# Four edits to a hybrid attention and GLA encoder kernel: norms stored as rows, a bank for P4, combines ahead of slots, and an alternating middle

## The chip, the cores and the metric

The kernel runs on one core of a Trainium2 chip. The metric is the device time in microseconds (us) of one launch. TensorE (PE in the profile) multiplies and accumulates into PSUM, of which this kernel uses eight banks; VectorE (DVE), ScalarE (ACT) and GpSimd (POOL) do the elementwise work; SyncE (SP) and GpSimd issue DMAs. Each engine works through its own queue in order.

## The reference

Two layers work on x of 512 tokens by 2048 features, all in fp32. Cut to what matters:

```python
def hybrid_layer(x, w_in, w_out, ...):
    z = rmsnorm(x, g_pre) @ w_in
    gq, gk, gv, gg, ga, aq, ak, av, ag = split_columns(z)   # GLA: q, k 512 wide, v, gate 1024; attention: 4 x 1024
    log_a = log_sigmoid(ga @ w_alpha + b_alpha) / 16
    o_gla = gla_chunk_causal(gq, gk, gv, log_a)             # 4 heads, state over 8 chunks of 64 tokens
    o_gla = rmsnorm(o_gla, g_gla) * silu(gg)                # per head
    o_att = chunk_band_attention(aq, ak, av, rel_bias)      # 8 heads, own chunk and the 8 before it
    o_att = rmsnorm(o_att, g_att) * silu(ag)                # per head
    y = concatenate([o_gla, o_att]) @ w_out
    return x + rmsnorm(y, g_post)
```

1/rms of a token multiplies the token's whole row of z, so the kernel multiplies unnormed x by the weights and applies 1/rms to the products later: as a number per partition where tokens lie on partitions, and as a row along the free dimension where features do.

## The kernel before

**Operands in two parts.** fp32 values are split in a high part that TensorE multiplies at full rate and a low part. For a chunk of weights, `high` casts the tile (`wh`, ScalarE, L195) and `low` subtracts (`wl`, VectorE, L199). Each product of two values is three matmuls: high by high, high by `wl`, low by `wh`.

**Pairs of output blocks.** Most of the two projections is done by `fast_gemm`, two output blocks of 512 columns at a time, by seven half-size products P1 to P7 in place of eight, each over four chunks of the inner dimension. A chunk of one product is 12 matmuls of 128x512. A layer has seven pairs: GG, AV, QK01 with QK23, QK45 with QK67, GK with GQ, GV, and, at the layer's end, the pair W23 (blocks 2 and 3 of the output projection), which is called the end pair here (`end=True`). The order of products is P1, P5, a middle of P6 and P3, P7, P2, P4; in the end pair P1, P2, P5, the middle, P7, P4. The other blocks (AG0, AG1, output blocks 0 and 1) go through `std_gemm`; output block 1 is done for the first 256 tokens before the end pair and for the others behind it.

**Banks.** A pair has two accumulators, X and Y, of two banks each (one per 128 tokens, `t`). P1, P6, P7 and P4 add into X; P5, P3 and P2 into Y, except in the end pair, where P2 has two auxiliary banks (Z). P1, P5 and P2 start a new sum (`starts`). After P1, P5 and P6 the accumulator is copied to SBUF on ScalarE (`copies`, L347 with 1/rms, L349 without). After P3, P7 and P2 a combine on VectorE (L356 with 1/rms, L358 and L360 without) reads the accumulator and one of the copies and gives a block of the result. P4 goes on adding to P7's sum in X, and that sum is its block of the result with no combine. In a pair of the usual order X is read by P7's combine while P2 runs; in the end pair P4 follows P7 at once.

**What the weights need first.** P5, P6 and the end pair's P4 add a loaded tile to the sum H (L190), P7 subtracts (L192), and P2 adds once more (L204), all on VectorE ahead of the cast. Weight tiles come through SyncE's queue into rings of four buffers (`raw`, `H`, `sa`, `wh`; `wl` has three).

**Tasks beside the stream.** The attention heads, GLA heads, sums and the next layer's preparation are tasks. `pace` runs pieces of them between products, and `until(condition)` runs them until a condition holds. The result of each block goes to a consumer: `kq_consume` for GK and GQ, `gv_consume` for GV. Both take slots in SBUF that are free only once certain attention heads are done, so they call `until` (head 6 and head 4), which emits those heads' instructions at this place. A scheduler orders each engine's instructions when the program is built; the order does not change afterwards.

**1/rms.** `token_norms` computes it for half of the tokens (two columns of 128 partitions), in GpSimd's power (L432), and stores each column to DRAM with a transfer of 128 single numbers on GpSimd's queue (L514), eight in all. `norm_row` reads the numbers back as a row, broadcast to all partitions, where features lie on partitions.

Of the kernel before, what the change touches and what calls it, by code (L numbers as in the profile page):

```python
# [11 lines left out]
ALU = mybir.AluOpType  # L12
# [3 lines left out]
P = 128  # L16
L = 2
S = 512
# [16 lines left out]
def hybrid_trunk(  # L35
# [65 lines left out]
    fac_d = [dram([P, 1024], f"fac{l}") for l in range(L)]  # L101
    r_d = [dram([S, 1], f"r{l}") for l in range(L)]

# [24 lines left out]
    W23 = (NB_IN + 2, NB_IN + 3)  # L128
    MIDDLE = [("P6", 0), ("P3", 0), ("P6", 1), ("P3", 1), ("P6", 2), ("P6", 3), ("P3", 2), ("P3", 3)]

# [199 lines left out]
    def fast_gemm(l, pair, consume, rate=0.0, skip=0, feature_major=False, after=None, end=False, scaled=True):  # L330
# [5 lines left out]
        if end:  # L336
            target["P2"] = "Z"
        prod = PROD_END if end else PROD
# [24 lines left out]
        def finished(k, t):  # L363
            x_, y_ = acc["X"][t], acc["Y"][t]
            if k == "P3":
                consume(1, 0, t, None, combine(y_, 0, t, keep["x"][t], 1, ALU.subtract))
            elif k == "P7":
                consume(1, 1, t, None, combine(x_, 1, t, keep["p5"][t], -1, ALU.add))
            elif k == "P2":
                consume(0, 0, t, None, combine(acc[target[k]][t], 0, t, keep["p1"][t], 1, ALU.add))  # L370
            elif k == "P4":
                consume(0, 1, t, x_, None)
# [31 lines left out]
        for k, c in prod:  # L404
# [5 lines left out]
            if c == 3:  # L410
                if k == "P1":
                    copies("p1", acc["X"])
                elif k == "P5":
                    copies("p5", acc["Y"])
                elif k == "P6":
                    copies("x", acc["X"])
                else:
                    for t in range(2):
                        finished(k, t)
            if after is not None:  # L420
                after(k, c)
# [80 lines left out]
    def token_norms(l, half, xs):  # L502
# [8 lines left out]
        nc.vector.tensor_tensor(out=norm[l][:, 2, cols], in0=ss, in1=r, op=ALU.mult)  # L511
        for j in range(2):
            t = 2 * half + j
            nc.gpsimd.dma_start(r_d[l][t * P : (t + 1) * P, :], inv_rms(l, t))  # L514
        normed.add((l, half))
        yield

    def norm_row(l, tok, n):
        z = t2((tok.stop - tok.start,))
        nc.sync.dma_start(z[0:n], r_d[l][tok, :].rearrange("s o -> o s").partition_broadcast(n))  # L520
        return z
# [140 lines left out]
    def layer(l):  # L662
# [26 lines left out]
        def forget_gate():  # L689
# [13 lines left out]
            until_normed(1)  # L703
            row = norm_row(l, slice(0, S), 96)
            nc.vector.tensor_tensor(out=raw[0:96, 1, :], in0=ps[0:96, :], in1=row[0:96, :], op=ALU.mult)
# [232 lines left out]
        def qk_consume(p):  # L938
            sets = {}

            def f(j, h, b, src, comb):
# [9 lines left out]
                else:  # L951
                    nc.vector.tensor_tensor(
                        out=z, in0=z, in1=norm_row(l, hs, P).unsqueeze(1).to_broadcast([P, 2, 256]), op=ALU.mult
                    )
# [25 lines left out]

        def kq_consume(j, h, t, src, comb):
            if j:
                if not gqT:
                    until(lambda: 6 in heads_done)
                    gqT.extend(slot(tag, [2, 512]) for tag in ("g12", "g13"))
                tasks.insert(0, transpose_q(2 * h + t, settled(src, comb)))
                return
            if not kdh:
                until(lambda: "done" in fgate)
                kdh.extend(slot(tag, [2, 512], F32R) for tag in ("g8", "g11"))  # L990
                kdl.extend(slot(tag, [2, 512], F32R) for tag in ("g14", "g15"))
            z = settled(src, comb)
            if comb is None:
# [166 lines left out]

        def gv_consume(j, h, t, src, comb):
            if (j, h) not in gvh:
                until(lambda: 4 in heads_done)
# [4 lines left out]
            else:  # L1168
                split(gvh[j, h][:, t, :], gvl[j, h][:, t, :], settled(src, comb))
            if h and t:  # L1170
# [176 lines left out]
```

## Time and profile before

| | |
|---|---|
| Median of 3 runs | 1682.63 us (1678.63 to 1688.18) |
| Profiled execution | 1680.65 us, of which the span 1678.9 |
| Mean granted TensorE clock | 0.994 |
| TensorE busy | 1635.4 us (97% of the span), 9026 matmuls and transposes |
| VectorE, ScalarE, GpSimd busy | 1223.9, 900.0, 173.8 us |
| DMA | 470.64 MB, mean 280 GB/s |

A row of the timeline reads: start in us from the span's beginning, duration, engine, line, operation, output and input tiles, shape, how many such instructions in a row; in brackets the idle time before it and what ended it. Matmuls are pipelined, so the duration of one (0.39 us for 128x512) is longer than the distance from one start to the next. A row of the waits reads: engine and line, what it waited for, total us, times, longest. A row of the stretches gives, for each engine, busy time and count, then the granted clock of TensorE, the mean busy share of the DMA engines, and GB/s.

### The profile page before, as it was taken

The numbers are of one execution on the slowest core, as the hardware profiler recorded it, in microseconds if no ns is written. First come the engines' busy times: TensorE is split into PE (matmuls) and PEld (weight loads), VectorE is DVE, ScalarE is ACT, GpSimd is POOL, SyncE is SP. The second block draws the span as 40 slices with busy tenths as digits, with TensorE's granted clock in tenths as the row PEclk, the third lists the DMA queues.
The fourth block names the chain that finished last, engine by engine and source line by source line (L and its number), as shares of the span: only waits on it lengthen the run. The fifth ranks groups of instructions, "written<-read, shape, count | busy, mean of one in ns | idle before, by whom it ended". The sixth has DMA issues, their size and how long they took to land.

```text
span 1678.9 us, 24925 instructions
## 1 busy us (share of the span) xinstructions
PE 1635.4 (97%) x9026; PEld 1396.3 (83%) x9026; DVE 1223.9 (73%) x1587; ACT 900.0 (54%) x1495; POOL 173.8 (10%) x264
## 2 busy tenths in 40 slices
PE   9999999999999999999999999999999999999987
PEld 7888889999987877687887878899999878776776
DVE  7567777877876885688785676768778677856875
ACT  7444544565666544554774454445666565435542
POOL 1210000000100101311121000000010001013101
PEclk9999999999999999999999999999999999999999
DMA  9988786858767787898799597968586778868984
GB/s 380 315 300 323 275 309 227 300 193 305 259 216 263 271 307 254 298 371 306 222 299 396 198 334 260 320 216 290 199 309 238 242 264 287 293 234 308 352 300 181
DMA packets 150683, 470.64 MB, mean 280 GB/s; under 512 B 16532, under 2 KB 35348, under 8 KB 150560
## 3 DMA queue, kind: packets, MB, share of 16 engines
q1 hardware_dynamic: 127408, 389.36, 67.3%
q0 software_dynamic: 22432, 78.41, 12.3%
q8 instruction: 71, 1.16, 0.3%
q10 hardware_dynamic: 720, 1.28, 0.2%
q14 instruction: 52, 0.43, 0.1%
HBM read 396.88 MB, written 72.11 MB: 279 GB/s over the span
## 4 chain that ended last, share of the span: by engine, by line
PE 82%; DMA 9%; DVE 5%; issue 2%; ACT 1%; POOL 0%; SPq 0%; DVEq 0%; ACTq 0%; POOLq 0%
PE mm L396 41%; PE mm L386 18%; PE mm L314 14%; DMA raw<-in_w_dram 3%; PE ax L865 2%; DVE wl L199 2%; DMA t<-fg 2%; DMA sa<-S 1%; DMA sg<-in_x_dram 1%; PE ax L1027 1%; PE ax L848 1%; DMA S<-g 1%; PE ax L696 1%; PE ax L1061 1%; DMA g<-in_x_dram 1%
## 5 line engine op out<-in xcount | busy, mean ns | idle before, releaser
L396 PE MATMUL mm<-wh,sa 128*128 128x512 f32 x1536 | 486.2, 392 | 3.1 <-DMA sa<-S 1.8
L195 ACT CAST wh<-raw 128x1024 fp32r<-128x1024 f32 x256 | 269.4, 1054 | 267.6 <-PE mm L396 98.8
L199 DVE TENSOR_TENSOR wl<-raw,wh 128x1024 fp32r<-128x1024 f32 x256 | 311.2, 1219 | 74.1 <-PE mm L396 19.5
L195 ACT CAST wh<-H 128x1024 fp32r<-128x1024 f32 x224 | 234.8, 1051 | 216.4 <-PE mm L396 114.7
L396 PEld LDWEIGHTS mm<-wh,sa 128*128 128x128 f32 x1536 | 288.1, 188 | 66.2 <-issue 4.9
L199 DVE TENSOR_TENSOR wl<-H,wh 128x1024 fp32r<-128x1024 f32 x224 | 272.6, 1220 | 90.2 <-PE mm L396 40.2
L396 PE MATMUL mm<-wl,sa 128*128 128x512 f32 x768 | 300.5, 391 | 4.6 <-DVE wl L199 4.6
L386 PE MATMUL mm<-sa,wh 128*128 128x256 f32 x1280 | 238.0, 285 | 0.0
L386 PEld LDWEIGHTS mm<-sa,wh 128*128 128x128 f32 x1280 | 200.3, 191 | 0.5
L396 PE MATMUL mm<-wh,a 128*128 128x512 f32 x576 | 183.9, 393 | 2.1 <-DVE t L356 2.1
L386 PE MATMUL mm<-sa,wl 128*128 128x256 f32 x640 | 181.3, 283 | 0.1
L314 PE MATMUL mm<-wh,a 128*128 128x512 f32 x512 | 171.3, 398 | 3.2 <-DVE g L1206 1.1
L396 PEld LDWEIGHTS mm<-wl,sa 128*128 128x128 f32 x768 | 144.3, 188 | 36.1 <-DVE wl L199 7.5
L190 DVE TENSOR_TENSOR H<-H,raw 128x1024 f32<-128x1024 f32 x120 | 145.8, 1220 | 10.0 <-DMA raw<-in_w_dram 8.3
L432 POOL TENSOR_TENSOR sm<-sm,mhalf 128x4 f32<-128x4 f32 (+2 forms) x40 | 58.4, 1459 | 708.7 <-DVE sm L875 458.9
L192 DVE TENSOR_TENSOR raw<-H,raw 128x1024 f32<-128x1024 f32 x56 | 68.6, 1225 | 84.2 <-DMA raw<-in_w_dram 84.0
L396 PEld LDWEIGHTS mm<-wh,a 128*128 128x128 f32 x576 | 107.3, 188 | 24.8 <-DVE t L356 2.4
L386 PEld LDWEIGHTS mm<-sa,wl 128*128 128x128 f32 x640 | 122.4, 191 | 0.4 <-DVE wl L199 0.3
L314 PEld LDWEIGHTS mm<-wh,a 128*128 128x128 f32 x512 | 96.8, 189 | 26.4 <-DVE g L1206 2.0
L396 PE MATMUL mm<-wl,a 128*128 128x512 f32 x288 | 112.6, 391 | 0.0
L314 PE MATMUL mm<-wl,a 128*128 128x512 f32 x256 | 101.2, 395 | 3.6 <-DVE wl L199 3.6
L386 PE MATMUL mm<-a,wh 128*128 128x256 f32 x512 | 94.7, 284 | 0.0
(202 smaller groups left out, 2349.6 us busy)
## 6 DMA issues: line engine op xcount, KB each, us to landing
raw<-in_w_dram SPq DMA_DIRECT2D x320, 512.0 KB, 5.4
sa<-S SPq DMA_DIRECT2D x192, 512.0 KB, 4.6
H<-in_w_dram SPq DMA_DIRECT2D x56, 512.0 KB, 4.6
sa<-A SPq DMA_DIRECT2D x48, 512.0 KB, 5.5
S<-g POOLq DMA_DIRECT2D x32, 512.0 KB, 8.8
oS<-g POOLq DMA_DIRECT2D x32, 512.0 KB, 6.4
sa<-oS SPq DMA_DIRECT2D x32, 512.0 KB, 5.3
sg<-t POOLq DMA_DIRECT2D x32, 256.0 KB, 6.0
```

The lines of the kernel that those rows point to most:

```text
L190: nc.vector.tensor_tensor(out=h, in0=h, in1=r, op=ALU.add)
L192: nc.vector.tensor_tensor(out=r, in0=h, in1=r, op=ALU.subtract)
L195: last_cast[0] = nc.scalar.copy(self.wh, src).ins
L199: last_low[0] = nc.vector.tensor_tensor(out=self.wl, in0=self.src, in1=self.wh.bitcast(F32), op=ALU.subtract).ins
L314: mm = nc.tensor.matmul(pss[o], a[:, part, t], rhs[:, kk, :], start=(i == 0 and kk == 0 and m == 0), stop=(i == n - 1 and kk == 1 and m == 2),
L386: nc.tensor.matmul(dst, lhs[:, kk, f], a[:, part, tok], start=(fresh and kk == 0 and m == 0 and ft % 2 == 0), stop=(c == 3 and kk == 1 and ...
L396: nc.tensor.matmul(out_ps[t], a[:, part, tok], rhs[:, kk, :], start=(fresh and kk == 0 and m == 0), stop=(c == 3 and kk == 1 and m == 2), ...
L432: nc.gpsimd.tensor_tensor(out=out_r, in0=v, in1=mhalf[:, : v.shape[-1]], op=ALU.pow)
L696: nc.tensor.matmul(ps[0:96, half * 256 : (half + 1) * 256], wga[kt // 10][:, kt % 10, :], op[:, i, (kt % 2) * 256 : (kt % 2 + 1) * 256], s ...
L848: nc.tensor.transpose(ps[:, j * P : (j + 1) * P], self.prob[i][:, j * P : (j + 1) * P], ident)
L865: nc.tensor.matmul(o, self.pt[i][:, j * P : (j + 1) * P], av[hd // 4, j // 2][:, j % 2, (hd % 4) * P : (hd % 4 + 1) * P], start=(j == 0), ...
L1027: nc.tensor.matmul(self.ps_u[cc][:, tt * 256 : (tt + 1) * 256], ops[cc][i][0], ops[cc][i][1], start=(i == 0), stop=(i == 2),)
```

## The change

There are four edits.

1. `token_norms` transposes the two columns of 1/rms on TensorE into a 2x128 tile in an auxiliary bank, copies it on VectorE to SBUF, and stores it with one transfer of two rows of 128 numbers: four transfers instead of eight. `norm_row` reads one or two halves, each with its own transfer.
2. In the end pair P4 starts a new sum in Y instead of adding to X. After P7 X is copied by ScalarE (two copies), and P4's block is made by a combine on VectorE (two) of Y and those copies.
3. `kq_consume` and `gv_consume` run the combine (`settled`) first, and only then call `until` and take their slots.
4. The middle goes P6 0, P3 0, P6 1, P3 1, P6 2, P3 2, P6 3, P3 3 in all pairs; before, it was P6 2, P6 3, P3 2, P3 3 in its second half.

```diff
-    r_d = [dram([S, 1], f"r{l}") for l in range(L)]
+    r_d = [[dram([2, P], f"r{l}{half}") for half in range(2)] for l in range(L)]
...
-    MIDDLE = [("P6", 0), ("P3", 0), ("P6", 1), ("P3", 1), ("P6", 2), ("P6", 3), ("P3", 2), ("P3", 3)]
+    MIDDLE = [(p, c) for c in range(4) for p in ("P6", "P3")]
...
         if end:
-            target["P2"] = "Z"
+            target.update(P2="Z", P4="Y")
+            starts.append("P4")
...
             elif k == "P2":
                 consume(0, 0, t, None, combine(acc[target[k]][t], 0, t, keep["p1"][t], 1, ALU.add))
+            elif k == "P4" and end:
+                consume(0, 1, t, None, combine(y_, 1, t, keep["x"][t], 1, ALU.add))
             elif k == "P4":
                 consume(0, 1, t, x_, None)
...
                     for t in range(2):
                         finished(k, t)
+                    if k == "P7" and end:
+                        copies("x", acc["X"])
...
-        for j in range(2):
-            t = 2 * half + j
-            nc.gpsimd.dma_start(r_d[l][t * P : (t + 1) * P, :], inv_rms(l, t))
+        ps = aux()
+        nc.tensor.transpose(ps[0:2, 0:P], r, ident)
+        row = t2((P,))
+        nc.vector.tensor_copy(row[0:2], ps[0:2, 0:P])
+        nc.gpsimd.dma_start(r_d[l][half], row[0:2])
...
-    def norm_row(l, tok, n):
-        z = t2((tok.stop - tok.start,))
-        nc.sync.dma_start(z[0:n], r_d[l][tok, :].rearrange("s o -> o s").partition_broadcast(n))
+    def norm_row(l, halves, n):
+        z = t2((256 * len(halves),))
+        for i, half in enumerate(halves):
+            nc.sync.dma_start(
+                z[0:n, i * 256 : (i + 1) * 256], r_d[l][half].rearrange("a b -> (a b)").partition_broadcast(n)
+            )
         return z
...
         def kq_consume(j, h, t, src, comb):
+            z = settled(src, comb)
             if j:
                 if not gqT:
                     until(lambda: 6 in heads_done)
                     gqT.extend(slot(tag, [2, 512]) for tag in ("g12", "g13"))
-                tasks.insert(0, transpose_q(2 * h + t, settled(src, comb)))
+                tasks.insert(0, transpose_q(2 * h + t, z))
                 return
...
-            z = settled(src, comb)
...
         def gv_consume(j, h, t, src, comb):
+            z = settled(src, comb)
             if (j, h) not in gvh:
                 until(lambda: 4 in heads_done)
...
-                split(gvh[j, h][:, t, :], gvl[j, h][:, t, :], settled(src, comb))
+                split(gvh[j, h][:, t, :], gvl[j, h][:, t, :], z)
```

How the edits move instructions is seen in the queues of three engines. The lines of the changed file lie 1 to 11 further down (L360 becomes L361, L1206 becomes L1217, L396 becomes L399). Tile names carry running numbers, which differ between the two programs.

VectorE in the end pair of layer 0, where P7 passes to P4. The first row is `wl` of P4's chunk 1; before:

```order
L199 TENSOR_TENSOR wl_7782<-H_7202,wh_7766 128x1024
L360 TENSOR_TENSOR t_1517_7808<-ev_7554,mm_7291 128x512
L199 TENSOR_TENSOR wl_7801<-H_7228,wh_7785 128x1024
L1206 TENSOR_TENSOR g_1518_7810<-t_1517_7808,t_1409_7289 128x512
L360 TENSOR_TENSOR t_1520_7814<-ev_7556,mm_7292 128x512
L1206 TENSOR_TENSOR g_1521_7816<-t_1520_7814,t_1409_7289 128x512
L199 TENSOR_TENSOR wl_7832<-H_7273,wh_7804 128x1024
L199 TENSOR_TENSOR wl_7856<-raw_7806,wh_7834 128x1024
```

and now:

```order
L199 TENSOR_TENSOR wl_7791<-H_7211,wh_7775 128x1024
L361 TENSOR_TENSOR t_1521_7817<-ev_7563,mm_7300 128x512
L199 TENSOR_TENSOR wl_7810<-H_7237,wh_7794 128x1024
L1217 TENSOR_TENSOR g_1522_7819<-t_1521_7817,t_1413_7298 128x512
L361 TENSOR_TENSOR t_1524_7823<-ev_7565,mm_7301 128x512
L199 TENSOR_TENSOR wl_7845<-H_7282,wh_7813 128x1024
L1217 TENSOR_TENSOR g_1525_7825<-t_1524_7823,t_1413_7298 128x512
L199 TENSOR_TENSOR wl_7869<-raw_7815,wh_7847 128x1024
L1243 SCALAR_TENSOR_TENSOR g_1358_7071<-g_1341_7013,sm_7854,g_1358_7071 128x1024
L1243 SCALAR_TENSOR_TENSOR g_1359_7072<-g_1453_7475,sm_7854,g_1359_7072 128x1024
L199 TENSOR_TENSOR wl_7893<-raw_7849,wh_7871 128x1024
L359 TENSOR_TENSOR t_1548_7923<-mm_7302,ev_7829 128x512
```

P7's two combines (L360, now L361) and P4's `wl` tiles keep their order, but the second L1206 now follows P4's last `wl`. The combine of P4 (L359) is new; it stands behind two `wl` tiles of output block 1 and two operations of the tokens' finish (L1243).

TensorE in the GK, GQ pair of layer 0, behind the last matmul of P7. L826 to L848 and L890 belong to attention heads; rows of L396 (L399) with an `a` operand are P2, chunk 0 (`a_22`), chunk 1 (`a_37`). Before:

```order
L826 MATMUL ax_5259<-g_778_4507,g_776_4505 128x256
L827 MATMUL ax_5259<-g_779_4508,g_776_4505 128x256
L828 MATMUL ax_5259<-g_778_4507,g_777_4506 128x256
L848 MATMUL ax_5270<-cst,t_946_5236 128x128 x4
L826 MATMUL ax_5277<-g_778_4507,g_776_4505 128x512
L827 MATMUL ax_5277<-g_779_4508,g_776_4505 128x512
L828 MATMUL ax_5277<-g_778_4507,g_777_4506 128x512
L848 MATMUL ax_5286<-cst,t_949_5245 128x128 x3
L890 MATMUL ax_5292<-cst,sg_5112 128x128 x4
L865 MATMUL ax_5306<-g_345_2042,t_959_5275 128x128 x2
L865 MATMUL ax_5306<-g_358_2120,t_959_5275 128x128 x2
L396 MATMUL mm_4733<-wh_5342,a_22_276 128x512
```

and now:

```order
L399 MATMUL mm_4742<-wh_5351,a_22_278 128x512
L399 MATMUL mm_4742<-wl_5374,a_22_278 128x512
L399 MATMUL mm_4742<-wh_5351,a_22_278 128x512 x2
L399 MATMUL mm_4742<-wl_5374,a_22_278 128x512
L399 MATMUL mm_4742<-wh_5351,a_22_278 128x512
L836 MATMUL ax_5270<-g_782_4516,g_780_4514 128x256
L837 MATMUL ax_5270<-g_783_4517,g_780_4514 128x256
L838 MATMUL ax_5270<-g_782_4516,g_781_4515 128x256
L399 MATMUL mm_4742<-wh_5377,a_37_347 128x512
L858 MATMUL ax_5281<-cst,t_951_5247 128x128 x4
L836 MATMUL ax_5288<-g_782_4516,g_780_4514 128x512
L837 MATMUL ax_5288<-g_783_4517,g_780_4514 128x512
```

P2's six matmuls of chunk 0 into its first bank now come ahead of the attention's, one of chunk 1 follows, and eleven more stand between the L858 with three matmuls and L900 (L890 before).

ScalarE in the AV pair of layer 0, around the copies of X after P6 (L347, now L348). The casts are, in order, of P3's chunks 2 and 3 and P7's chunks 0 to 3. Before:

```order
L195 CAST wh_1932<-raw_1870 128x1024
L195 CAST wh_1950<-raw_1895 128x1024
L195 CAST wh_1971<-raw_1952 128x1024
L347 ACTIVATE ev_1998<-mm_1706,norm_204 128x512
L195 CAST wh_1992<-raw_1973 128x1024
L347 ACTIVATE ev_2000<-mm_1707,norm_204 128x512
L195 CAST wh_2017<-raw_1994 128x1024
L195 CAST wh_2038<-raw_2019 128x1024
```

and now, from P6's chunk 3, P3's chunk 3 and P7's chunk 0 on:

```order
L195 CAST wh_1941<-H_1684 128x1024
L195 CAST wh_1959<-raw_1922 128x1024
L195 CAST wh_1980<-raw_1961 128x1024
L195 CAST wh_2001<-raw_1982 128x1024
L348 ACTIVATE ev_2028<-mm_1715,norm_206 128x512
L195 CAST wh_2022<-raw_2003 128x1024
L348 ACTIVATE ev_2030<-mm_1716,norm_206 128x512
L195 CAST wh_2047<-raw_2024 128x1024
```

The two copies stood behind P7's first cast and now have two casts of P7 ahead of them; the cast between the copies is that of P7's chunk 2 (before, chunk 1).

More of the change, by code (lines that the diff above doesn't have):

```diff
@@ L703, in forget_gate @@
             until_normed(1)
-            row = norm_row(l, slice(0, S), 96)
+            row = norm_row(l, (0, 1), 96)
             nc.vector.tensor_tensor(out=raw[0:96, 1, :], in0=ps[0:96, :], in1=row[0:96, :], op=ALU.mult)
@@ L952, in f @@
                     nc.vector.tensor_tensor(
-                        out=z, in0=z, in1=norm_row(l, hs, P).unsqueeze(1).to_broadcast([P, 2, 256]), op=ALU.mult
+                        out=z, in0=z, in1=norm_row(l, (h,), P).unsqueeze(1).to_broadcast([P, 2, 256]), op=ALU.mult
                     )
```

## The prediction

> **What bounds the kernel now.** I read the busy shares first, then what TensorE waited for, then the timelines and stretches around those waits. "P6 2" is chunk 2 of product P6. From the page, busy time and share of the span:
>
> ```profile
> PE 1635.4 (97%) x9026; PEld 1396.3 (83%) x9026; DVE 1223.9 (73%) x1587; ACT 900.0 (54%) x1495; POOL 173.8 (10%) x264
> ```
>
> TensorE is the bound: no edit takes matmuls away, so the change can only win what TensorE stands still, or runs at a lower clock. The rows of TensorE's waits that this change can touch (total us, times, longest):
>
> ```profile
> PE mm L396 <- DVE t L360: 8.2, 2, 4.1
> PE mm L396 <- DVE wl L199: 4.6, 6, 1.3
> PE mm L314 <- DVE wl L199: 3.6, 2, 3.1
> PE ax L890 <- ACT t L851: 2.7, 2, 1.4
> PE mm L396 <- DVE t L356: 2.1, 2, 1.0
> PE mm L396 <- DMA sa<-S: 1.8, 2, 1.0
> PE mm L314 <- ACT t L669: 1.1, 1, 1.1
> ```
>
> The first row is the largest: twice 4.1 us, once in each layer. In the end pair P4 adds onto P7's sum in X, so it must wait until VectorE has read X for P7's block (L360). TensorE's timeline of layer 0 there, the start in layer 1, then three stretches (us; busy of PE, PEld, DVE, ACT, POOL with counts; granted clock; DMA share; GB/s):
>
> ```profile
> 791.19 0.39 PE L396 MATMUL mm<-wh,sa 128*128 128x512 f32 x1
> 795.68 0.77 PE L396 MATMUL mm<-wh,g 128*128 128x512 f32 x1 [4.10 <-DVE t L360]
> 796.24 0.63 PE L396 MATMUL mm<-wl,g 128*128 128x512 f32 x1
> ...
> 1634.60 0.76 PE L396 MATMUL mm<-wh,g 128*128 128x512 f32 x1 [4.14 <-DVE t L360]
> ...
> 788.00:796.00 8.00, 3.90 (x17) 2.98 (x16) 8.00 (x10) 3.73 (x6) 7.43 (x5) 0.89 1.01 397
> 796.00:802.00 6.00, 6.00 (x17) 4.66 (x17) 2.56 (x4) 1.01 (x4) 0.00 (x0) 0.58 0.81 327
> ...
> 1635.00:1642.00 7.00, 7.00 (x20) 5.44 (x20) 2.48 (x4) 0.93 (x4) 0.00 (x0) 0.59 0.65 263
> ```
>
> P7's last matmul starts at 791.19 and P4's first at 795.68; VectorE is busy for all 8.00 us around it. After the wait the clock is at 0.58: the wait is paid again in slow matmuls. At full clock, 24 matmuls took 5.51 us in this row of the chain of waits, so 0.23 us each and 2.75 for a chunk of 12:
>
> ```profile
> 575.73 5.51 PE mm L396 x24
> ```
>
> **A. P4 in its own bank.** What goes: the two waits, 8.2. The slow stretches: 17 matmuls in 6.00 us instead of 3.91 (2.1 too much), 20 in 7.00 instead of 4.60 (2.4), and each first matmul, 795.68 to 796.24, 0.33 too long (0.7). Together 13.4. What is late next is VectorE itself:
>
> ```profile
> 790.32 1.21 DVE L199 TENSOR_TENSOR wl<-H,wh 128x1024 fp32r<-128x1024 f32 x1
> 791.45 2.35 DVE L190 TENSOR_TENSOR H<-H,raw 128x1024 f32<-128x1024 f32 x2
> 793.72 1.22 DVE L199 TENSOR_TENSOR wl<-H,wh 128x1024 fp32r<-128x1024 f32 x1
> 794.86 0.68 DVE L360 TENSOR_TENSOR t<-ev,mm 128x512 f32<-128x512 f32 x1
> 795.46 1.22 DVE L199 TENSOR_TENSOR wl<-H,wh 128x1024 fp32r<-128x1024 f32 x1
> ```
>
> These are the low parts of P4 0, P4 1 and P4 2, and the order of the change keeps all five rows in this place. P4 0 could start at 791.42; its second matmul needs wl at 791.65 and has it at 791.53. P4 1 would start at 794.17 and need wl at 794.40; it comes at 794.94, 0.5 late. P4 2 would need it at about 797.7 and has it at 796.68. The two added copies of X on ScalarE (0.7 each by the L347 rows below) run beside P4, where ScalarE was busy 1.01 of 6.00. The two added combines on VectorE (0.68 by the L360 row) stand among the low parts of output block 1's second half, which follows P4; VectorE has 3.4 of 6.00 free from 796, but the backlog arrives earlier now, and I allow 0.5 a layer. So 1.0 a layer comes back. Bounds: 13.4 gained, or, if half of each wait stays (2.0) with a slow stretch of 2.4 behind it, about 4.6. I take 13.4 - 2.0 = **-11.4**, since the low parts are rows with known ends.
>
> Whether a short wait slows the clock is the open point. The rows speak both ways:
>
> ```profile
> 1530.55 0.89 PE L1089 MATMUL ax<-cst,sg 128*128 128x128 f32 x4 [1.87 <-issue]
> ...
> 1531.00:1535.00 4.00, 4.00 (x12) 3.17 (x13) 1.04 (x2) 0.25 (x2) 1.66 (x4) 0.57 1.02 329
> ```
>
> Here the clock fell to 0.57 behind a wait of only 1.87, which several shorter ones preceded. The expected 0.5 stands alone, so I charge no slow stretch. The Trainium skill, in "TensorE: Matmul & The Clock Gate", Part 1, says that the clock halves after about one idle window of some 3.4 us. By it A is -11.4 as well, and even a remaining wait of 2 us would cost only itself; the stretch at 1531 differs from it, so it does not bound rival 2.
>
> **B. Combines ahead of slots.** In the GK, GQ pair the combine of P3's first bank is queued behind attention heads, and P2 cannot enter Y before it. Layer 0, TensorE and then VectorE (two rows):
>
> ```profile
> 516.57 0.63 PE L848 MATMUL ax<-cst,t 128*128 128x128 f32 x4 [1.00 <-DVE sg L879]
> 519.66 0.66 PE L890 MATMUL ax<-cst,sg 128*128 128x128 f32 x4 [1.36 <-ACT t L851]
> 522.25 0.50 PE L396 MATMUL mm<-wh,a 128*128 128x512 f32 x1 [1.03 <-DVE t L356]
> ...
> 511.03 1.23 DVE L204 TENSOR_TENSOR H<-H,raw 128x1024 f32<-128x1024 f32 x1 [3.09 <-DMA raw<-in_w_dram]
> 521.44 1.41 DVE L356 SCALAR_TENSOR_TENSOR t<-mm,norm,ev 128x512 f32<-128x512 f32 x2
> ```
>
> TensorE has nothing but attention between P7 and P2, and waits three times; layer 1 has two of the three (the rows with L851 and L356 count two each). Waits: 1.0 + 2.7 + 2.1 = 5.8. The change puts the first bank's combine before the attention steps, and its order has 18 matmuls of P2 between them: 6, 1 and 11, or 4.1 us, against waits of 3.4. The combine itself moves into VectorE's idle 3.09 before 511.03. The second bank's combine stays behind the attention, but its matmuls come only after the first bank's. Bounds: 5.8 gained, nothing gained if the waits reappear at the next heads, which have 18 matmuls fewer beside them. I take **-5.2**. The same move in the GV pair removes no wait that the rows show: 0.
>
> **C. 1/rms as rows.** A half is stored by two transfers (L514) of 128 single numbers. First L514's landing times and its first and last start; then two stretches, two pieces of the chain, and a start on TensorE:
>
> ```profile
> L514 POOL DMA_DIRECT2D r<-norm x8: 537/542/600, 38.3 to 872.3; - x8
> DMA to landing us min/median/max: 9.6/11.8/15.8
> ...
> 45.00:50.00 5.00, 5.00 (x24) 4.14 (x23) 0.79 (x2) 0.26 (x2) 0.53 (x1) 1.00 0.74 79
> 880.00:885.00 5.00, 4.44 (x20) 3.35 (x18) 0.10 (x1) 1.80 (x3) 0.00 (x0) 1.00 0.99 186
> 885.00:890.00 5.00, 2.49 (x11) 2.04 (x12) 4.97 (x7) 3.40 (x6) 1.18 (x3) 1.00 1.02 415
> ...
> 33.57 16.20 DMA sg<-in_x_dram
> 869.64 14.53 DMA S<-g
> ...
> 887.51 0.50 PE L314 MATMUL mm<-wl,a 128*128 128x512 f32 x1 [3.07 <-DVE wl L199]
> ```
>
> About ten us after these stores start, the DMA engines are busy for most of the time (0.74, 0.99) but move 79 and 186 GB/s, where 415 follows at the same share. Loads that straddle this take 16.20 and 14.53 us, and the matmuls behind them wait 1.1 (the L669 row) and 3.07: 4.2 in all. With four stores of two 512-byte rows instead of eight of single numbers I expect the engines to stay free. Added: four transposes, by the four matmuls of the L848 row at most 0.63 us together; four copies of 2x128 on VectorE, shorter than any row above; two more reads of the row on SyncE's queue, long after the store. The transposes wait for 1/rms on GpSimd, with the matmuls of AG0 queued behind; if the x rows stay late, the second would wait. Bounds: 4.2 gained to about 3 lost. I take -4.2 + 0.6 = **-3.6**, nearest to the two chain rows.
>
> **D. Alternating to the end.** P6 3 comes one chunk (2.75) later. In GV it waits for an operand (1.8 for both layers), which the chunk covers if the load does not move with it: 1.8 gained or 0; I take 1.5. Against it, in the GK, GQ pairs the subtraction for P7 1 (L192), which waits for a load, now stands ahead of the low part of P6 2; where that order exists already, part of the "mm L396, wl L199" row arises, 0.8 a time (4.6 over 6). I charge 0.4. New in all 14 pairs: X is copied after P6 3, and P7 enters X one chunk later, not two. The copies of the second pair, on ScalarE:
>
> ```profile
> 218.58 0.69 ACT L347 ACTIVATE ev<-mm,norm 128x512 f32<-128x512 f32 x1 [0.99 <-PE mm L396]
> 219.25 1.05 ACT L195 CAST wh<-raw 128x1024 fp32r<-128x1024 f32 x1
> 220.21 0.68 ACT L347 ACTIVATE ev<-mm,norm 128x512 f32<-128x512 f32 x1
> ...
> DVE raw L192 <- DMA raw<-in_w_dram: 84.0, 47, 4.5
> ```
>
> The first copy starts when the first bank is done; the second bank is done three matmuls later, 219.3, and copied by 220.9: 1.6. P7 needs it 2.75 + 0.7 = 3.4 after. Slack 1.8, cost 0; without it, rival 4. D: **-1.1**.
>
> **Sum.** -11.4 - 5.2 - 3.6 - 1.1 = -21.3 against the profiled execution's own 1680.65 us (span 1678.9, 1.75 around it): 1659.4. The median of the runs, 1682.63, is 2.0 higher, so **1661 us**.
>
> **Rivals.**
> 1. *The stores are innocent of the slow stretches.* For it: the loads of x rows and operands crowd the same places. Against: busy engines that move little, in both layers. C becomes +0.6 to +3: about 1667.
> 2. *VectorE, not the bank, is the limit in the end pair.* For it: 8.00 of 8.00 busy. A wait of 2.0 stays in each layer and the clock falls as at 1531: A is -4.6, 1668. Against: the five rows, whose ends do not depend on P4.
> 3. *The waits of B go to the next heads.* The chain of softmax steps sets the end of the pair, and P2's matmuls are missing there later. B is 0: 1666.
> 4. *Slower: the second copy of X is late.* In its queue it stands behind the cast of P7 2, which waits for L192, which waits for a load (84.0 us over 47, at most 4.5). If that is 4.5 late in every pair, 4.5 - 1.8 = 2.7 for 14 pairs is 38 lost, net +17: about 1699. It decides once L192 is over 1.8 + 21.3 / 14 = 3.3 late in all pairs. Against: the mean is 1.8, those waits lie ahead of need, and the copies of Y, which have one chunk already (before P3), appear in no row of TensorE's waits.
>
> **How the numbers follow.** Forecast 0.55, rivals 0.14, 0.15, 0.12 and 0.04. Everything gained is 13.4 + 5.8 + 4.2 + 1.8 = 25.2, 1657; the lowest run lies 4 below the median, so the range starts at 1652. Rivals 1 and 2 together give 1674: it ends at **1675**. A measurement of this kernel tells about 0.5%, 8.4 us, from no change: faster is below 1674. All of the forecast, most of rivals 1 to 3 and few mixtures fail that: faster 0.87, same 0.09, slower 0.04.
>
> **What would show it.** A: no L360 in TensorE's waits; the clock at 1.00 behind P7 of the end pair; a wait of about 0.5 for wl in P4 1. B: matmuls of P2 between those of attention, the rows with L851 and L356 gone. C: landing of the row stores far below 9.6 us, no stretch of some 100 GB/s at a full DMA share, AG0's waits gone. D: the "sa<-S" row gone and no wait of P7 0 for the copies. Wrong it would be if TensorE waits for casts or copies at the head of P7 in most pairs, or if the clock stays low in P4.

## The result

The changed kernel takes 1669.65 us (median of 8 runs, 1665.77 to 1676.13) against 1679.64 us for the kernel before in the same comparison: ratio 0.9941, 95% interval 0.9914 to 0.9968. By the ratio that is 9.9 us faster, where 21.3 us were forecast. The time lies in the range, but less than half of the expected gain arrived. The profiled execution (1674.78 us, span 1673.0) is 5 us above the median of its runs, so its stages are read one by one below.

TensorE's waits in the changed kernel (total us, times, longest):

```profile
PE mm L399 <- DVE wl L199: 5.6, 8, 1.3
PE mm L399 <- ACT wh L195: 2.7, 3, 1.7
PE mm L389 <- DVE wl L199: 2.5, 4, 0.9
PE mm L399 <- DMA sa<-S: 2.2, 2, 1.2
PE ax L836 <- DVE sg L889: 1.9, 2, 1.0
PE ax L875 <- ACT t L881: 1.8, 2, 0.9
PE mm L314 <- DVE wl L199: 0.5, 1, 0.5
```

The two waits of 4.1 us behind P7's combine are gone, and so is the pair of rows of the GK, GQ pair (L851 and L356 before). AG0's wait for `wl` fell from 3.6 to 0.5. The rows for casts and low parts of `fast_gemm` grew: `wh` from 1.0 to 2.7, `wl` from 4.6 to 5.6, and there is a new row of 2.5 in the QK pairs (L389). GV's operand wait, `sa<-S`, did not go; it now stands at another chunk.

Where P7 passes to P4 in the end pair, the clock is whole (stretches; busy by engine, granted clock, DMA share, GB/s):

```profile
802.00:810.00 8.00, 8.00 (x36) 6.50 (x35) 8.00 (x10) 3.75 (x6) 7.67 (x5) 1.00 1.01 394
1628.00:1634.00 6.00, 6.00 (x28) 4.99 (x27) 6.00 (x8) 3.15 (x3) 6.00 (x2) 1.00 1.01 402
```

In the GK, GQ pair P2 follows P7's last matmul at once, and one new wait stands at a later attention step:

```profile
523.64 0.39 PE L399 MATMUL mm<-wh,sa 128*128 128x512 f32 x1
523.87 0.39 PE L399 MATMUL mm<-wh,a 128*128 128x512 f32 x1
...
532.43 0.94 PE L875 MATMUL ax<-g,t 128*128 128x128 f32 x6 [0.89 <-ACT t L881]
```

The stores of 1/rms land in less than half the time (median 5.1 us, 11.8 before):

```profile
L521 POOL DMA_DIRECT2D r<-t x4: 511/536/553, 44.6 to 882.1; - x4
DMA to landing us min/median/max: 2.9/5.1/9.0
```

Some ten us behind the first and the last of these stores, where the busy DMA engines moved 79 and 186 GB/s before, they now move 333 and 409 (just before the first of these, from 50 to 55, they are busy for 0.46 and move 147):

```profile
55.00:60.00 5.00, 5.00 (x23) 4.13 (x22) 3.76 (x8) 2.40 (x4) 2.91 (x6) 1.00 0.90 333
890.00:895.00 5.00, 5.00 (x26) 4.19 (x25) 4.16 (x6) 2.40 (x4) 1.60 (x3) 1.00 1.01 409
```

What was lost shows in the end pair itself, in P5 of layer 0, which had a single wait of 0.4 us before:

```profile
760.11 0.73 PE L399 MATMUL mm<-wh,sa 128*128 128x512 f32 x2 [0.60 <-ACT wh L195]
761.37 0.50 PE L399 MATMUL mm<-wl,sa 128*128 128x512 f32 x1 [0.53 <-DVE wl L199]
765.59 0.73 PE L399 MATMUL mm<-wh,sa 128*128 128x512 f32 x2 [1.65 <-ACT wh L195]
767.30 0.50 PE L399 MATMUL mm<-wl,sa 128*128 128x512 f32 x1 [0.98 <-DVE wl L199]
```

### The profile page after: what moved, and what is told of

Same layout as the page of the kernel before. It is cut to its first block, busy times and chain, and to the rows that moved or that the text cites. A ratio compares the mean times of both kernels' runs of the same rounds, so it can differ in the third digit from the quotient of the medians.

```text
span 1673.0 us, 24933 instructions
## 1 busy us (share of the span) xinstructions
PE 1635.7 (98%) x9030; PEld 1393.8 (83%) x9030; DVE 1225.3 (73%) x1595; ACT 900.2 (54%) x1499; POOL 176.3 (11%) x260
## 3 DMA queue, kind: packets, MB, share of 16 engines
q0 software_dynamic: 22304, 78.41, 12.3%
## 4 chain that ended last, share of the span: by engine, by line
PE 65%; DMA 5%; DVE 2%; issue 2%; ACT 1%; POOL 0%; SPq 0%; DVEq 0%; ACTq 0%; POOLq 0%
PE mm L399 33%; PE mm L314 14%; PE mm L389 10%; DMA raw<-in_w_dram 2%; DMA t<-fg 2%; PE ax L875 2%; PE ax L1037 1%; DVE wl L199 1%; PE ax L858 1%; DMA sa<-S 1%; PE ax L1071 1%; PE ax L836 0%; PE ax L838 0%; PE ax L837 0%; PE ax L706 0%
## 5 line engine op out<-in xcount | busy, mean ns | idle before, releaser
L399 PE MATMUL mm<-wh,sa 128*128 128x512 f32 x1536 | 486.6, 392 | 5.4 <-ACT wh L195 2.7
L195 ACT CAST wh<-raw 128x1024 fp32r<-128x1024 f32 x256 | 269.2, 1055 | 273.2 <-PE mm L399 125.0
L399 PEld LDWEIGHTS mm<-wh,sa 128*128 128x128 f32 x1536 | 287.7, 188 | 69.5 <-ACT wh L195 5.6
L399 PE MATMUL mm<-wl,sa 128*128 128x512 f32 x768 | 301.2, 392 | 5.6 <-DVE wl L199 5.6
L389 PE MATMUL mm<-sa,wh 128*128 128x256 f32 x1280 | 237.0, 285 | 0.0
L389 PEld LDWEIGHTS mm<-sa,wh 128*128 128x128 f32 x1280 | 199.9, 191 | 0.4
L399 PE MATMUL mm<-wh,a 128*128 128x512 f32 x576 | 184.5, 391 | 0.0
L389 PE MATMUL mm<-sa,wl 128*128 128x256 f32 x640 | 181.7, 284 | 1.2 <-DVE wl L199 1.2
L399 PEld LDWEIGHTS mm<-wl,sa 128*128 128x128 f32 x768 | 144.3, 188 | 38.7 <-DVE wl L199 9.9
L437 POOL TENSOR_TENSOR sm<-sm,mhalf 128x4 f32<-128x4 f32 (+2 forms) x40 | 64.2, 1604 | 701.5 <-DVE sm L885 462.8
L399 PEld LDWEIGHTS mm<-wh,a 128*128 128x128 f32 x576 | 108.1, 188 | 22.1
L389 PEld LDWEIGHTS mm<-sa,wl 128*128 128x128 f32 x640 | 122.4, 191 | 1.8 <-DVE wl L199 1.6
L399 PE MATMUL mm<-wl,a 128*128 128x512 f32 x288 | 113.4, 394 | 0.1
L389 PE MATMUL mm<-a,wh 128*128 128x256 f32 x512 | 94.8, 284 | 0.0
```

Source lines behind the costliest of these rows:

```text
L195: last_cast[0] = nc.scalar.copy(self.wh, src).ins
L389: nc.tensor.matmul(dst, lhs[:, kk, f], a[:, part, tok], start=(fresh and kk == 0 and m == 0 and ft % 2 == 0), stop=(c == 3 and kk == 1 and ...
L399: nc.tensor.matmul(out_ps[t], a[:, part, tok], rhs[:, kk, :], start=(fresh and kk == 0 and m == 0), stop=(c == 3 and kk == 1 and m == 2), ...
L437: nc.gpsimd.tensor_tensor(out=out_r, in0=v, in1=mhalf[:, : v.shape[-1]], op=ALU.pow)
```

## The experiments

Twelve kernels were run, each against the kernel before. Single stages are compared by the distance from the first matmul of a stage to that of the next one, worked out from the timelines (us, one profiled execution each). The first two rows run from P7 of GK, GQ to P5 of GV. The last four are longer: from P7 of GK, GQ to GV's last matmul, the whole end pair and the two QK pairs (each with both layers added up), and from the end pair of layer 0 to layer 1's first pair, GG:

| stage | before | change | e1 | e2 | e3 | e4 | e5 | e6 | e7 | e8 | e9 | e10 | e11 | e12 |
|---|---|---|---|---|---|---|---|---|---|---|---|---|---|---|
| GK,GQ to GV, layer 0 | 61.1 | 58.2 | 58.2 | 60.3 | 60.3 | 58.2 | 60.0 | 58.2 | 58.2 | 58.2 | 58.2 | 60.2 | 58.2 | 58.1 |
| GK,GQ to GV, layer 1 | 60.1 | 58.2 | 58.2 | 60.3 | 59.9 | 58.2 | 60.1 | 58.2 | 58.1 | 58.2 | 58.2 | 60.3 | 58.2 | 60.1 |
| end pair P5, layer 0 | 11.6 | 16.0 | 16.8 | 11.7 | 11.4 | 17.0 | 11.6 | 11.9 | 15.3 | 13.4 | 12.9 | 12.1 | 13.4 | 11.7 |
| end pair P5, layer 1 | 13.6 | 13.4 | 18.0 | 13.6 | 12.2 | 12.3 | 14.0 | 13.3 | 12.2 | 12.2 | 10.9 | 12.8 | 11.8 | 11.7 |
| end pair P7 (to P4), layer 0 | 15.1 | 11.7 | 10.9 | 14.0 | 10.9 | 13.7 | 13.4 | 10.9 | 10.9 | 10.9 | 10.9 | 12.6 | 12.7 | 10.9 |
| end pair P7 (to P4), layer 1 | 16.4 | 10.9 | 10.9 | 13.9 | 11.0 | 14.1 | 15.0 | 10.9 | 12.2 | 10.9 | 10.9 | 13.1 | 12.0 | 10.9 |
| QK01,QK23 P7, layer 0 | 11.5 | 11.5 | 11.5 | 13.2 | 11.5 | 11.5 | 11.5 | 11.6 | 11.5 | 13.4 | 11.5 | 11.7 | 11.5 | 11.5 |
| QK45,QK67 P2, layer 0 | 13.8 | 16.1 | 13.8 | 13.9 | 13.8 | 13.8 | 13.8 | 13.8 | 13.8 | 14.6 | 13.8 | 13.8 | 13.8 | 13.7 |
| GK,GQ P7 to GV's end | 269.3 | 266.4 | 266.2 | 270.8 | 268.3 | 267.0 | 268.4 | 266.6 | 266.6 | 266.3 | 266.4 | 269.2 | 267.0 | 270.8 |
| end pair, whole | 175.2 | 165.5 | 170.2 | 172.1 | 159.4 | 171.9 | 170.3 | 160.3 | 164.7 | 160.8 | 158.8 | 163.7 | 163.0 | 158.5 |
| QK pairs, whole | 382.2 | 389.5 | 381.7 | 384.5 | 382.4 | 382.0 | 381.7 | 383.1 | 381.7 | 387.8 | 382.2 | 381.9 | 381.7 | 383.5 |
| end pair to GG, layer 1 | 127.5 | 124.2 | 124.2 | 130.4 | 129.4 | 127.7 | 124.4 | 124.1 | 132.4 | 124.1 | 124.1 | 129.4 | 127.0 | 124.1 |

Without any wait P5 and P7 of the end pair take 10.9 us.

### First question: which edit gave less, or cost?

**The change with the old middle (e1).**

```diff
-    MIDDLE = [(p, c) for c in range(4) for p in ("P6", "P3")]
+    MIDDLE = [("P6", 0), ("P3", 0), ("P6", 1), ("P3", 1), ("P6", 2), ("P6", 3), ("P3", 2), ("P3", 3)]
```

> The change with the old middle (P6 2, P6 3, P3 2, P3 3 at its end); the other three edits stay. Theory one, the alternating middle gives about 9 us back to waits for low parts and attention in the GG, AV and QK pairs, while the other edits gained what the forecast said: about 1660 us, ratio to the kernel before 0.988. Theory two, the middle is neutral and one of the other edits gained less than forecast: like the change, ratio 0.994.

Measured: 1670.83 us, ratio 0.9941 (0.9920 to 0.9962), the change's own ratio. So theory one failed here: taking the new middle out of the change gave nothing back. Its table column shows another loss: P5 of the end pair takes 16.8 and 18.0.

**The new middle alone (e2).** The same two lines, put into the kernel before.

> The kernel before with the alternating middle alone. Theory one: slower by 6 to 9 us, ratio 1.004 to 1.005, and waits of VectorE's wl on TensorE in GG, AV and both QK pairs that the kernel before does not have. Theory two: within 2 us, ratio 0.999 to 1.001. The forecast's own step: 1 us faster.

Measured: ratio 1.0022 (1.0004 to 1.0041), 3.7 us slower: between the two theories, and against the forecast's sign. Its new waits (the group, and the two rows of layer 0) are in the QK pairs:

```profile
PE mm L386 <- DVE wl L199: 1.0, 2, 0.7
...
309.21 0.39 PE L386 MATMUL mm<-sa,wl 128*128 128x256 f32 x1 [0.67 <-DVE wl L199]
312.69 0.39 PE L386 MATMUL mm<-sa,wl 128*128 128x256 f32 x1 [0.34 <-DVE wl L199]
```

VectorE just before, first in the kernel before, then with the new middle:

```profile
303.32 1.22 DVE L199 TENSOR_TENSOR wl<-raw,wh 128x1024 fp32r<-128x1024 f32 x1
304.45 0.68 DVE L358 TENSOR_TENSOR t<-mm,ev 128x512 f32<-128x512 f32 x1
305.05 1.21 DVE L204 TENSOR_TENSOR H<-H,raw 128x1024 f32<-128x1024 f32 x1
306.19 1.22 DVE L199 TENSOR_TENSOR wl<-raw,wh 128x1024 fp32r<-128x1024 f32 x1
```

```profile
304.14 1.22 DVE L199 TENSOR_TENSOR wl<-raw,wh 128x1024 fp32r<-128x1024 f32 x1
306.20 1.23 DVE L204 TENSOR_TENSOR H<-H,raw 128x1024 f32<-128x1024 f32 x1 [0.84 <-DMA raw<-in_w_dram]
307.34 0.69 DVE L358 TENSOR_TENSOR t<-mm,ev 128x512 f32<-128x512 f32 x1
307.94 1.22 DVE L199 TENSOR_TENSOR wl<-raw,wh 128x1024 fp32r<-128x1024 f32 x1
```

P2's addition (L204), which waits for its load, now stands ahead of P3's combine and the next low part; the low part starts 1.75 us later (0.82 of it was there in the low part before), and TensorE waits for it.

**The P4 bank alone (e3).** The lines of the second edit in the diff, put into the kernel before.

> The kernel before with P4 of the end pair in its own bank alone. Theory one and the forecast: 11 to 13 us faster, ratio 0.992 to 0.993, the waits on L360 and the slow clock in P4 gone. Theory two, if this is the edit that gained less: 5 us, ratio 0.997, with waits for wl and a clock still low in P4.

Measured: 1667.25 us, ratio 0.9920 (0.9899 to 0.9940), 13.4 us faster. P7 to P4 takes 10.9 and 11.0 instead of 15.1 and 16.4, and the slow clock behind it is gone. By itself this edit gains 13.4 us (10.1 to 17.0) where all four together gain 9.9 (5.4 to 14.4); the intervals overlap, but no gain of the other three is seen on top.

**The combines ahead of slots alone (e4).** The third edit of the diff (`kq_consume`, `gv_consume`) in the kernel before.

> The kernel before with the combines ahead of slots alone. Theory one and the forecast: about 5 us faster, ratio 0.997, with the three waits of the GK, GQ pair in layer 0 and the two of layer 1 gone. Theory two, if this is the edit that gained less: no difference, and waits of the same size at later attention steps of the same pair.

Measured: ratio 0.9984 (0.9964 to 1.0003), 2.7 us. Its own stage gained about what was forecast: 2.9 us in layer 0 and 1.9 in layer 1. But half of it is gone at the end of the next pair: up to GV's last matmul 2.3 us are left (269.3 and 267.0). P5 of the end pair, over 200 us later, went from 11.6 to 17.0 in layer 0.

### Second question: why is P5 of the end pair slow where the combines were moved?

SyncE's queue tells. Before (L147 loads a weight tile, L180 an operand, which needs the GLA output's store `oS` to have landed; start, time at issue):

```profile
733.28 0.33 SPq L147 DMA_DIRECT2D raw<-in_w_dram  x1
735.37 0.33 SPq L180 DMA_DIRECT2D sa<-oS  x1
735.79 0.44 SPq L147 DMA_DIRECT2D raw<-in_w_dram  x1
736.33 0.94 SPq L180 DMA_DIRECT2D sa<-oS  x2
738.08 5.55 SPq L147 DMA_DIRECT2D raw<-in_w_dram  x4
```

and in e4:

```profile
736.49 0.33 SPq L147 DMA_DIRECT2D raw<-in_w_dram  x1
737.91 0.86 SPq L180 DMA_DIRECT2D sa<-oS  x2
738.92 0.38 SPq L147 DMA_DIRECT2D raw<-in_w_dram  x1
739.38 0.44 SPq L180 DMA_DIRECT2D sa<-oS  x1
741.29 8.82 SPq L147 DMA_DIRECT2D raw<-in_w_dram  x4
```

The moved combines shifted the steps of the tasks, and the scheduler put a second operand load ahead of the weight load of P5's chunk 1. That load started at 735.79 and starts at 738.92 in e4. Its start isn't held up by the operand loads: in both kernels it follows, by 0.11 and 0.03 us, the end of the low part of P2's chunk 1 on VectorE, which by the ring of four frees its buffer, and the weight load ahead of all these operand loads starts 3.2 us later too. What the place in the queue goes with is the landing. VectorE's sum for chunk 1 waits for this load, before and in e4:

```profile
742.05 1.23 DVE L190 TENSOR_TENSOR H<-H,raw 128x1024 f32<-128x1024 f32 x1 [1.21 <-DMA raw<-in_w_dram]
748.53 1.23 DVE L190 TENSOR_TENSOR H<-H,raw 128x1024 f32<-128x1024 f32 x1 [3.36 <-DMA raw<-in_w_dram]
```

The sum starts 6.3 us after the load's start before, and 9.6 in e4. Over all kernels and both layers it is 9.3 to 10.7 us with two operand loads right ahead, 6.3 to 7.9 with one, and 5.6 to 7.2 in the kernels below that put the weight loads first. P2's combines and the other sums stand behind this one on VectorE, and the casts of P5 come late:

```profile
756.44 0.73 PE L396 MATMUL mm<-wh,sa 128*128 128x512 f32 x2 [1.64 <-ACT wh L195]
758.16 0.63 PE L396 MATMUL mm<-wl,sa 128*128 128x512 f32 x1 [0.99 <-DVE wl L199]
```

In layer 0 this place in the queue goes with the combines in every kernel: with it P5 takes 15.3 to 17.0 (change, e1, e4, e7), without it 11.4 to 11.7 (before, e2, e3, e5). Part of it is the clock, which fell behind these waits in e1, e4 and e7 and not in the change. In P5 of e1:

```profile
760.00:765.00 5.00, 5.00 (x15) 3.96 (x14) 5.00 (x6) 2.27 (x3) 0.00 (x0) 0.60 0.54 184
```

It stood at 0.50 for 6.8 us there and for 3.4 in e4 and e7, which costs, by estimate, half of that. The remedy tried: in the end pair each operand load is issued behind the last weight load.

```diff
-                nc.sync.dma_start(flat(self.a), src)
+                with tc.issue_after(last_load[0]) if end else nullcontext():
+                    nc.sync.dma_start(flat(self.a), src)
```

**Three edits with the weight loads first (e6):** e1 with these lines.

> The change with the old middle, and in the end pair each operand load (sa from oS) is issued behind the weight load of its chunk. Theory three: the combines ahead of slots move an operand load, which waits for the output's store, ahead of a weight load in SyncE's queue, and P5 of the end pair then takes 16.8 us in layer 0 and 18.0 in layer 1 instead of 11.6 and 13.6. With the weight loads first P5 should take 11 to 13 in both, and the time be 6 to 9 us below the same kernel without this edit: about 1662 us, ratio 0.990. Rival (the DMA engines are full there, whatever the order): P5 stays at 16 to 18, ratio 0.994.

Measured: 1660.23 us, ratio 0.9877 (0.9853 to 0.9901), 20.7 us below the kernel before, where e1 is 9.9 below it. P5 takes 11.9 and 13.3 instead of 16.8 and 18.0, 9.6 less in all. Of these, by estimate, 6.8 are the slow clock of e1, 3.4 in each layer, which did not fall in P5 of e6. SyncE's queue at the same place:

```profile
733.78 0.33 SPq L147 DMA_DIRECT2D raw<-in_w_dram  x1
734.16 0.45 SPq L181 DMA_DIRECT2D sa<-oS  x1
736.20 0.33 SPq L147 DMA_DIRECT2D raw<-in_w_dram  x1
736.63 0.45 SPq L181 DMA_DIRECT2D sa<-oS  x1
738.57 0.33 SPq L147 DMA_DIRECT2D raw<-in_w_dram  x1
```

The weight load of chunk 1 starts no earlier than in e1, 10.7 us before P5's first matmul against 10.6, but the sum starts 5.7 us after it (e1: 9.8). So the order that theory three names matters, but by the landing of the weights; a wait for the store ahead of their issue isn't seen.

**The control (e10):** the same lines in the kernel before, nothing else.

> The kernel before with the weight loads first in the end pair, nothing else: the control for that edit. Theory three: P5 of the end pair took 11.6 and 13.6 before, so at most 1 to 3 us are to be had, ratio 0.9985 to 1.000. If it gains 6 us or more by itself, the edit's gain says nothing on the combines.

Measured: ratio 0.9950 (0.9930 to 0.9969), 8.4 us faster by itself. That is outside what theory three allowed, and by the expectation's own words e6's gain alone then proves nothing on the combines. The table shows where it comes from. P5 hardly moves (12.1 and 12.8); P7 to P4 falls to 12.6 and 13.1, because the wait that the P4 bank removes is shorter (that earlier weights let VectorE reach P7's combine earlier is argued, not shown):

```profile
793.13 0.47 PE L397 MATMUL mm<-wh,g 128*128 128x512 f32 x1 [1.60 <-DVE t L361]
```

with no low clock behind it in the profile. In e6 this part cannot be gained again, because P4 waits for that combine in neither e1 nor e6 (P7 takes 10.9 in both).

**Combines with the weight loads first (e11).**

> The kernel before with the combines ahead of slots and the weight loads first. Theory three: the combines' 4.9 us in the GK, GQ pair come through, and what the control gains besides: ratio 0.995 to 0.997, P5 of the end pair at 11 to 13 us in layer 0 instead of 17.0. Rival (the combines are worth 2 to 3 us, wherever the loads stand): 0.998 times the control.

Measured: ratio 0.9936 (0.9914 to 0.9959), 0.9986 times the control. The rival's number came, not theory three's. P5 of layer 0 fell from 17.0 to 13.4, short of 11 to 13. So the order of the loads explains the bulk of P5's loss by its stages, but that the combines are worth 5 us once the loads are in order is not shown by the times, whose intervals of 0.2% each can't exclude it. The stages speak for the rival: up to GV's last matmul e11 is 2.2 us ahead of the control (267.0 and 269.2).

**P4 bank and combines (e7).** The second and the third edit of the diff in the kernel before.

> The kernel before with the P4 bank and the combines ahead of slots, without the other two edits. Theory three: the bank's 11 to 13 us, the combines' 5 in the GK, GQ pair, and 5 lost in P5 of the end pair: ratio 0.992 to 0.993. If P5 of layer 0 stays at 11 to 12 us, theory three is wrong about where its cause lies.

Measured: ratio 0.9937 (0.9914 to 0.9960), 10.6 us, a little less than expected, though the expected ratios lie in the interval; P5 of layer 0 takes 15.3, as theory three needs.

**1/rms as rows alone (e5).** The first edit of the diff (`r_d`, `token_norms`, `norm_row`) in the kernel before.

> The kernel before with 1/rms stored as rows alone. The forecast: 3 to 4 us faster, ratio 0.998, the wait of 3.07 us in AG0 of layer 1 gone. Rival (this edit takes back what the others gain, since the three edits without the middle gave less than the P4 bank alone): 2 to 4 us slower, ratio 1.001 to 1.003, with new waits in the first 100 us or in AG0 of layer 1.

Measured: ratio 0.9976 (0.9962 to 0.9989), 4.0 us faster. The rival fell, and the wait of 3.07 us in AG0 of layer 1 is gone from its profile.

### Third question: what does the alternating middle cost, and where?

**The whole change with the weight loads first (e8).**

> The change, whole, with the weight loads first in the end pair. Theory three: P5 of the end pair at 11 to 13 us in both layers, 4 to 8 us below the change, ratio 0.989 to 0.991. If the alternating middle costs some us of its own, as it did alone (ratio 1.0022), it is slower than the same kernel with the old middle by 2 to 5 us; if not, the two are equal.

Measured: 1665.52 us, ratio 0.9905 (0.9884 to 0.9926), 5.3 us above e6 in the same comparison, which differs by the middle alone. P7 of the first QK pair in layer 0 takes 13.4, and the QK pairs together 387.8 instead of 383.1.

**Alternating everywhere but in the QK pairs (e9).**

```diff
-            stream += [Job(l, k, c, b0, b1, pr) for k, c in PROD]
+            stream += [Job(l, k, c, b0, b1, pr) for k, c in (PROD_QK if b0 in (QK01, QK45) else PROD)]
...
-        prod = PROD_END if end else PROD
+        prod = PROD_END if end else PROD_QK if feature_major else PROD
```

> As the change whole with the weight loads first (ratio 0.9905), but the two QK pairs of each layer keep the old middle. Theory four: the cost of the alternating middle lies mostly in the QK pairs, whose P7 takes 13.2 to 13.4 us instead of 11.5 and P2 up to 1 us longer: 3 to 5 us faster than with all pairs alternating, ratio 0.988. Rival (the cost lies in the other pairs, GG, AV and GV): no faster than 0.9905. The forecast's own place for a cost, P6 2 of the GK, GQ pair, would show there and nowhere else.

Measured: 1658.68 us, ratio 0.9881 (0.9862 to 0.9901), level with e6: alternating costs in the QK pairs, and elsewhere no cost was seen beyond the intervals of 0.2%. P7 of the first QK pair is back at 11.5 us in both layers, and the QK pairs together at 382.2. e6 and e9 are both faster than the change and the kernel before.

**Weight loads first in all pairs (e12):** e6 without the words `if end else nullcontext()`.

> As the three edits without the alternating middle and with the weight loads first (ratio 0.9877), but the weight loads come first in all pairs. If operand loads ahead of weight loads cost elsewhere too, 1 to 3 us faster; if the operands themselves are what comes late, as in the GV pair's P6 3, which waits 1 to 1.6 us for its operand in each layer, slower by 1 to 4 us.

Measured: 1667.28 us, ratio 0.9923 (0.9896 to 0.9950), worse than e6 by 7 us. `sa<-S` in its waits (2.0) is no longer than in e6 (2.6), so the expected mechanism isn't seen; the GK, GQ pair's P2 in layer 1 took 20.3 us instead of 18.3, and GV from P7 to its end 41.2 instead of 40.2 in both layers; why stays open.

## Why the prediction came out as it did

**A, P4 in its own bank: right.** Forecast -11.4, measured alone -13.4 (-17.0 to -10.1). The waits and the slow stretches went. The 0.5 us wait for P4 1's low part did not show in the change (P4's stretches are busy throughout); VectorE, busy for 8.00 of 8.00 us as before, was no new bound. Rival 2 fell.

**B, combines ahead of slots: right at its place, wrong as a whole.** The stage gained 4.8 us (2.9 and 1.9) where 5.2 were forecast, with 0.9 of each layer's gain already given back at the next head (the L875 row), a small share of rival 3. Alone, the edit gave 2.7. Two steps failed. The move in the GV pair was put at 0, since it removes no wait. But with the same matmuls in another order GV takes 40.2 us from P7 to its end instead of 39.6, in each layer, and up to there only 2.3 to 2.9 us of the gain are left (e4, the change). And the bound "nothing gained if the waits reappear at the next heads" looked for the loss on TensorE and at the attention steps only. The edit moves tasks, tasks move loads in SyncE's queue, and P5 of the end pair paid 4 to 5 us in layer 0. In e4 the end pair as a whole is not longer for it (171.9 against 175.2), since P4's wait and the slow clock behind it are shorter there; with the bank in place it is 5.3 longer (e7 and e3: 164.7 and 159.4). That queue was counted for the row reads of C, not for B.

**C, 1/rms as rows: right.** Forecast -3.6, measured -4.0 (-6.4 to -1.8). Landing fell from a median of 11.8 us to 5.1, and the wait of 3.07 went. The stage around it, from the end pair to layer 1's GG, takes 124.1 to 124.4 us in every kernel with the rows and 127.0 to 132.4 in every one without; so the busy engines that move little went with the stores, and rival 1 fell. The other part, the wait of 1.1 in layer 0 (L669), hardly went: it is 0.8 in the change and in e5. And the chain's row of 14.53 us, read as a load, is a store of operands (`S<-g`).

**D, alternating to the end: wrong in sign.** Forecast -1.1, measured alone +3.7 (+0.7 to +6.9), and +5.3 on top of e6. Two steps failed. GV's wait did not go. P6 3 itself, a chunk later, no longer waits, as the forecast had it; but P3 2 now runs a chunk earlier, in its place, and waits for its own operand, which the forecast did not look at. In the change, layer 0:

```profile
596.25 0.47 PE L399 MATMUL mm<-wh,sa 128*128 128x512 f32 x1 [1.23 <-DMA sa<-S]
```

And the cost was sought in P6 2 of GK, GQ (0.4) and in X's copies. The copies were not late: no row of TensorE's waits names them, as the slack of 1.8 had it, so rival 4's mechanism did not occur. The order of VectorE's work around L204 in the QK pairs was not looked at: these pairs take 2.3 us more with D alone (384.5 and 382.2), and 7.3 more in the change.

**The sum.** Without D the forecast's terms give -20.2, and e6, which has those three edits and the loads in order, measures -20.7. That agreement is partly luck, since A's term is 2.0 us too small by its own measurement and B's 2.5 too large. The four edits alone sum to -13.4 - 2.7 - 4.0 + 3.7 = -16.4, and the change gives -9.9 (-14.4 to -5.4). The table shows where the gain went, in one execution each: the end pair of the change takes 6.1 us more than with the bank alone (165.5 and 159.4), and the QK pairs 7.3 more than before (389.5 and 382.2). The forecast had put P5 and the QK pairs at nothing. With the measured A and C and B's 2.9 up to GV's end that is -13.4 - 4.0 - 2.9 + 6.1 + 7.3 = -6.9, where the two profiled executions differ by -5.9.

Why then did removing D from the change (e1) gain nothing? The QK pairs gave back 7.8 us, but the end pair took 4.7 more (170.2), 4.5 of it in P5 of layer 1, where the clock fell to 0.50 for 6.8 us; in the change it fell in neither P5. This isn't that one execution alone: over e1's six runs the mean clock was 0.993 to 0.996, over the change's eight 0.996 to 0.998. The clock also answers why the kernel before and e5, which have the same two loads swapped in layer 1, pay only 13.6 and 14.0 there: it did not fall, and their sum for chunk 1 starts 1.4 and 1.0 us ahead of P5, where that of the change in layer 0 starts 1.1 behind P5's first matmul (16.0). Why the clock falls in one kernel's P5 and not in the other's stays open.

## What to carry to other kernels

Where a scheduler orders queues, an edit of the program's order is priced only when every in-order queue has been compared over the whole layer, the DMA queue above all. An operand load put ahead of a weight load that is needed sooner made the weights land later (9.6 us instead of 6.3), though it did not delay their issue. Compare a gain up to the end of the next stages, not at its own place alone: of B's 4.8 us half was gone one pair later. Test edits of a bundle singly: here one of the four by itself gained 13.4 us, the bundle 9.9, and another cost. A bank of its own for a product that would otherwise wait for the reader of the last one was worth 13.4 us where the waits were 8.2, since the slow clock behind them went too.

## What was unexpected of the hardware

The granted clock fell behind short waits, and not in each execution. At the turn from GV to the output projection the same row appears in both kernels; with TensorE's wait, the stretch behind it in the kernel before (layer 0) and in the change:

```profile
696.49 0.89 PE L1089 MATMUL ax<-cst,sg 128*128 128x128 f32 x4 [1.89 <-issue]
697.00:702.00 5.00, 4.42 (x20) 3.31 (x20) 2.36 (x4) 2.52 (x8) 1.59 (x4) 1.00 0.99 390
```

```profile
704.53 1.25 PE L1099 MATMUL ax<-cst,sg 128*128 128x128 f32 x4 [1.88 <-issue]
705.00:710.00 5.00, 4.67 (x15) 3.50 (x15) 1.50 (x3) 1.18 (x4) 1.63 (x4) 0.69 1.00 387
```

The waits are equal, the clock is 1.00 in one and 0.69, the mean over the stretch, in the other; in layer 1 the two kernels change sides. Over the profiles of before, the change and e1 to e11 it fell in 16 of 26 such turns. "TensorE: Matmul & The Clock Gate", Part 1, of the Trainium skill speaks of an idle window of about 3.4 us that is free-running; the free-running part would fit these rows, but no single wait here reaches that length. In these profiles the granted clock is either 1.00 or 0.50, and up to the last pair's end each fall lasts 3.4 or 6.8 us, so that one costs, by estimate, 1.7 or 3.4. That is one source of the spread of several us between runs of the same kernel, whose mean clock went from 0.990 to 0.997 in the kernel before.
